# Convolution blocks inside the attention steps, up-projections ahead of the gating, low parts on VectorE: a two-layer trunk on one core

## The chip, the cores and the metric

The kernel runs on one core of one Trainium2 chip. The metric is the device time of one execution in microseconds; a lower time is better. TensorE (PE in the profile) multiplies matrices and loads weights (PEld), VectorE is DVE, ScalarE is ACT, GpSimd is POOL, SyncE (SP) issues the DMAs.

## What is computed

Two layers of one trunk run over 256 latent and 256 context tokens of 1024 features. Each layer has a half-step feed-forward block, a mixing stage and a second half-step feed-forward block, each behind an RMS norm with shift, scale and gate. The change lies in the mixing stage, which joins three groups:

```python
q_lat, kv_lat, k_pe, sg_in, cv_in = jnp.split(hn @ w_mix_in[l], splits, axis=-1)
q = mla_queries(q_lat, ...)                # rms_norm, up-projection, norm per head, rope
k, v = mla_keys_values(kv_lat, k_pe, ...)  # the same for keys; values
attn = latent_attention(q, k, v, kc, vc)   # 8 heads, 256 queries on 512 keys
sg = spatial_gating(sg_in, ...)            # gelu, norm of v by groups, w_spatial @ v + b, times u
cv = short_conv(cv_in, w_conv[l])          # b * conv3(c * x)
y = jnp.concatenate([rms_norm(attn, ...), rms_norm(sg, ...), rms_norm(cv, ...)], axis=-1)
h = h + mod_l[5] * (y @ w_mix_out[l])
```

In layer 0 the context tokens go through the same steps with their own attention (256 queries on 256 keys); in layer 1 they give keys and values alone.

## The kernel before

**Products.** All large products take their operands in two parts, high and low (`whi`, `wlo`, `xh`, `xl`), and three matmuls per product (`mm3` with weights stationary, L384 to L386, `mm3x` with tokens stationary, L389 to L391). They go to PSUM tiles of the tag `mm`, of which there are six; two more, `sm`, serve transposes and small sums.

**Weights.** The class `Weights` streams all weights in the order of their use. A load brings a raw tile; `pump` makes the high part on ScalarE (L125) and the low part (L126) on the engine that `W.low` names: "g" is GpSimd, "v" VectorE, "a" both in turn. Five pairs of parts exist (`SUBB`); a new one is prepared when the prefix of finished weights (`sub_pref`) allows. `SPARE` is room of one pair that attention uses for itself. `W.hold` stops preparation except where `W.pump(1)` asks for one. `W.low` is "g" from the end of the first feed-forward block to the start of the second.

**Order.** The schedule is the program's order on each engine (`manual_schedule`); semaphores are placed by data dependencies and by the reuse of tiles. A mixing stage runs: latents of keys and queries (`kv_lat`, `kv_ctx`, in layer 0 `q_ctx`), `k_prep` (rotation of the shared key part), `uv_lat` and `uv_ctx` (gating inputs; their end emits `v_norm`, the norm of the gating's v, tile by tile: square on ScalarE, sums on VectorE, square root on ScalarE, four scalings on VectorE, high part on ScalarE, low part on VectorE). Then conv blocks 0 to 3, `spatial`, conv blocks 4 and 5, `y_sg` (transposed gated features), `k_up`, `y_cv_stats` (statistics of the convolution's norm), `q_up`, `y_cv` (the normalised convolution). A conv block is 24 matmuls of 512 columns in layer 0 and 256 in layer 1; kinds 0, 1 and 2 (c, x, b) are evacuated by a ScalarE copy, by a product and three convolution operations on VectorE, and by a product with a square.

**Attention** is twelve steps `att(i)`. Step i makes the scores of head i-2 (`B`: maxima and bias on VectorE, exponentials on ScalarE, normalisation on GpSimd), the transposed probabilities of head i-3 (`C`), products with the values (`Dv`, two heads at a time) and the transposed queries and keys of head i (`A`). Step 0 begins with `v_up`; its evacuations (`v_evac`) follow in steps 1 and 2. Steps 9 to 11 begin the output projection (`mo_begin`), which needs the features of the gating and the convolution.

`k_up` evacuates a tile with one step's delay: `fin` of tile t follows the square root of tile t+1, and frees the tile's bank.

Of the kernel before, what the change touches and what calls it, by code (L numbers as in the profile page):

```python
# [39 lines left out]
# packed per-partition parameters: name -> columns for one layer  # L40
# [20 lines left out]
class Weights:  # L61
    """Streams weights in order: DRAM -> raw tile -> (high, low) float32r parts, ahead of their use.
    SPARE in the stream is room of one weight, left to other uses between its take and its done."""

    def __init__(self, nc, pool, raws):
# [18 lines left out]
        self.sub_fin = [False] * len(self.subs)  # L84
        self.sub_pref = 0
# [7 lines left out]
    def pump(self, preps=None):  # L93
        """Start the loads that have room, and prepare the parts (at most preps, when held back)."""
# [3 lines left out]
        while go:  # L98
# [8 lines left out]
            while left > 0 and self.prep_i < len(self.subs) and self.prep_i < self.sub_pref + SUBB:  # L107
# [67 lines left out]
def hybrid_trunk_kernel(ctx: ExitStack, tc: tile.TileContext, io: dict, out: bass.AP):  # L175
# [65 lines left out]
    # ---------------------------------------------------------------- weight specs  # L241
# [110 lines left out]
    def split_norm(src, dst_h, dst_l, rb, a, b=None, eng=None):  # L352
        """high and low parts of src * a * rb (+ b); returns the emission of the low part."""
# [17 lines left out]
    def staggered(makers):  # L371
        """runs emissions that return a follow-up, each follow-up one later"""
# [60 lines left out]
    # ---------------------------------------------------------------- FFN  # L433
    def ffn(l, which, ntok, tail, first=None):
        """tail(part): called by the last block to start the chain of what follows."""
# [28 lines left out]
        def first_two(W):  # L464
            """Blocks 0 and 1: the latent half while the norm of the context half is under way."""
# [147 lines left out]
    def boundary(l, i):  # L613
        """tail of the last block before norm i of layer l: work(0..2) is the ctx half in three parts."""
# [18 lines left out]
    # ---------------------------------------------------------------- mixing  # L633
    def mixing(l):
# [5 lines left out]
        def open_pools(W):  # L640
# [9 lines left out]
            st["row"] = per.tile([128, NROW], F32, name="row")  # L650
            SP.dma_start(out=st["row"], in_=io["row"][:, l])
            P["kvh"] = per.tile([128, 2, NTOK], F32R, name="kvh")
            P["kvl"] = per.tile([128, 2, NTOK], F32R, name="kvl")
# [9 lines left out]
            P["stok"] = P["guv"][:, :, 0:256]  # L663
            P["cvo"] = p1.tile([128, 2, NQ], F32, name="cvo")
# [948 lines left out]
```

## Time and profile before

| | us |
|---|---|
| median of 3 runs | 1778.43 |
| range of the runs | 1777.52 to 1781.66 |
| profiled execution (its span; the page gives no other time of it) | 1778.8 |

| engine | busy us | share of the span |
|---|---|---|
| TensorE, matmul | 1715.4 | 96% |
| TensorE, weight load | 1450.0 | 82% |
| VectorE | 1077.7 | 61% |
| ScalarE | 661.1 | 37% |
| GpSimd | 328.9 | 18% |

Layer 0's mixing stage lies between about 406 and 650 us of the span, layer 1's between about 1403 and 1580. A view of stretches gives, for each piece of the span, how long every engine was busy in it; a busy time below the length is waiting. The granted clock of TensorE stands beside it, 1.00 for 2.4 GHz and 0.50 for 1.2 GHz. The order in time gives single instructions, with the idle time before one and what ended it in the last brackets.

### The profile page before, as it was taken

How to read it: one execution, taken by the hardware profiler on the slowest of the kernel's cores; microseconds unless marked ns; L12 is line 12 of the kernel's file. 1: busy time of each engine (PE TensorE's matmuls, PEld its weight loads, DVE VectorE, ACT ScalarE, POOL GpSimd, SP SyncE). 2: the span in 40 equal slices, each digit the busy share in tenths (PEclk: the TensorE clock that was granted, in tenths of full speed). 3: DMA queues.
4: the chain of work that ended last, by engine and by line, in shares of the span. 5: the costliest groups of instructions: out<-in, count | busy, mean ns of one | idle time of the engine just before them, and what ended most of it. 6: DMA issues, size and time to landing. Idle time of an engine off the chain costs nothing.

```text
span 1778.8 us, 24162 instructions
## 1 busy us (share of the span) xinstructions
PE 1715.4 (96%) x9422; PEld 1450.0 (82%) x9422; DVE 1077.7 (61%) x1778; ACT 661.1 (37%) x1124; POOL 328.9 (18%) x210
## 2 busy tenths in 40 slices
PE   8999999999998999999999999999999987889999
PEld 6888888889876688888888888888888986589999
DVE  5667777635578475575766356576765577554332
ACT  4422223224457443222232242222222355554442
POOL 0000000004346522000000030000000165465442
PEclk9999999999999999999999999999999998899999
DMA  8545555523211124454555234454454242136553
GB/s 318 189 158 181 184 182 191 178 84 98 82 60 48 37 70 151 134 176 155 165 175 166 98 107 158 162 164 161 158 174 123 70 142 69 36 116 210 185 180 94
DMA packets 71395, 248.59 MB, mean 140 GB/s; under 512 B 8048, under 2 KB 9584, under 8 KB 71280
## 3 DMA queue, kind: packets, MB, share of 16 engines
q1 hardware_dynamic: 71136, 246.97, 42.3%
q8 instruction: 74, 1.21, 0.3%
q14 instruction: 41, 0.34, 0.1%
q10 hardware_dynamic: 144, 0.07, 0.0%
HBM read 245.96 MB, written 1.05 MB: 139 GB/s over the span
## 4 chain that ended last, share of the span: by engine, by line
PE 87%; DVE 7%; ACT 3%; issue 2%; POOL 1%; DMA 1%; ACTq 0%; POOLq 0%; DVEq 0%
PE mm L384 26%; PE mm L385 25%; PE mm L386 25%; PE mm L389 2%; PE mm L391 2%; PE mm L390 2%; PE sm L288 1%; ACT p L1130 1%; PE sm L1181 1%; DVE mx L1119 1%; PE mm L1363 1%; DMA raw<-in_w_ada 1%; DVE xl L361 1%; PE sm L1076 1%; PE mm L1158 1%
## 5 line engine op out<-in xcount | busy, mean ns | idle before, releaser
L384 PE MATMUL mm<-xh,whi 128*128 128x512 f32 (+1 forms) x1712 | 612.0, 358 | 6.5 <-DVE kvl L723 3.1
L385 PE MATMUL mm<-xl,whi 128*128 128x512 f32 (+1 forms) x1712 | 605.7, 354 | 4.0 <-DVE xl L361 3.4
L386 PE MATMUL mm<-xh,wlo 128*128 128x512 f32 (+1 forms) x1712 | 604.1, 353 | 1.8 <-POOL wlo L126 1.3
L125 ACT ACTIVATE whi<-raw 128x1024 fp32r<-128x1024 f32 (+1 forms) x334 | 339.1, 1020 | 486.3 <-PE mm L385 373.6
L126 POOL TENSOR_TENSOR wlo<-raw,whi 128x1024 fp32r<-128x1024 f32 (+3 forms) x112 | 258.1, 2318 | 1335.7 <-ACT whi L125 1320.3
L126 DVE TENSOR_TENSOR wlo<-raw,whi 128x1024 fp32r<-128x1024 f32 (+2 forms) x222 | 265.9, 1199 | 244.8 <-ACT whi L125 244.8
L384 PEld LDWEIGHTS mm<-xh,whi 128*128 128x128 f32 x1712 | 327.4, 191 | 63.9 <-issue 11.8
L385 PEld LDWEIGHTS mm<-xl,whi 128*128 128x128 f32 x1712 | 327.4, 191 | 48.2 <-DVE xl L361 4.5
L386 PEld LDWEIGHTS mm<-xh,wlo 128*128 128x128 f32 x1712 | 327.4, 191 | 45.6 <-POOL wlo L126 1.5
L278 DVE SCALAR_TENSOR_TENSOR scratch<-raw,cs,scratch 128x512 f32<-128x512 f32 x448 | 307.4, 745 | 0.0
L384 PE MATMUL mm<-gh,whi 128*128 128x512 f32 (+1 forms) x770 | 270.2, 351 | 0.0
L386 PE MATMUL mm<-gh,wlo 128*128 128x512 f32 (+1 forms) x770 | 267.1, 347 | 0.0
L385 PE MATMUL mm<-gl,whi 128*128 128x512 f32 (+1 forms) x770 | 267.0, 347 | 0.0
L454 ACT ACTIVATE gh<-sa 128x512 fp32r<-128x512 f32 (+1 forms) x88 | 50.9, 579 | 310.2 <-DVE sa L453 310.2
L384 PEld LDWEIGHTS mm<-gh,whi 128*128 128x128 f32 x770 | 145.8, 189 | 22.3 <-issue 4.9
L386 PEld LDWEIGHTS mm<-gh,wlo 128*128 128x128 f32 x770 | 145.8, 189 | 18.3
L385 PEld LDWEIGHTS mm<-gl,whi 128*128 128x128 f32 x770 | 145.9, 189 | 17.5
L276 DVE TENSOR_SCALAR scratch<-raw,cs 128x512 f32<-128x512 f32 x64 | 28.2, 484 | 148.9 <-PE sm L288 148.9
L455 DVE TENSOR_TENSOR gl<-sa,gh 128x512 fp32r<-128x512 f32 (+1 forms) x88 | 57.7, 656 | 56.8 <-ACT gh L454 56.8
L453 DVE TENSOR_TENSOR sa<-sa,mm 128x512 f32<-128x512 f32 (+1 forms) x88 | 53.9, 613 | 17.7 <-PE mm L386 16.0
L408 DVE TENSOR_TENSOR acc<-acc,sq 128x256 f32<-128x256 f32 x63 | 41.4, 657 | 35.1 <-ACT sq L407 35.1
L360 ACT ACTIVATE xh<-scratch,mods 128x256 fp32r<-128x256 f32 x88 | 42.8, 506 | 52.9 <-DVE scratch L356 52.9
(207 smaller groups left out, 1457.6 us busy)
## 6 DMA issues: line engine op xcount, KB each, us to landing
raw<-in_w_ffn_in SPq DMA_DIRECT2D x176, 512.0 KB, 3.9
raw<-in_w_ada SPq DMA_DIRECT2D x144, 512.0 KB, 4.2
raw<-in_w_ffn_out SPq DMA_DIRECT2D x64, 512.0 KB, 4.4
raw<-in_w_ffn_out SPq DMA_DIRECT2D x32, 384.0 KB, 3.4
raw<-in_w_mo SPq DMA_DIRECT2D x16, 512.0 KB, 3.5
raw<-in_w_cv SPq DMA_DIRECT2D x12, 512.0 KB, 3.7
raw<-in_w_uv SPq DMA_DIRECT2D x8, 512.0 KB, 3.9
raw<-in_w_q SPq DMA_DIRECT2D x8, 384.0 KB, 3.1
```

What stands on the lines that cost most here:

```text
L125: nc.scalar.activation(hi[:, a:b], src, AF.Copy)
L126: eng.tensor_tensor(lo[:, a:b], src, hi[:, a:b].bitcast(F32), ALU.subtract)
L278: DVE.scalar_tensor_tensor(acc[:, s], src, cv, acc[:, s], ALU.mult, ALU.add)
L360: ACT.activation(dst_h, u, AF.Identity, bias=b)
L384: PE.matmul(bank, lhsT=wh, rhs=xh, start=first, stop=False)
L385: PE.matmul(bank, lhsT=wh, rhs=xl, start=False, stop=False)
L386: PE.matmul(bank, lhsT=wl, rhs=xh, start=False, stop=last)
L389: PE.matmul(bank, lhsT=xh, rhs=wh, start=first, stop=False)
L408: DVE.tensor_tensor(acc[:, half], acc[:, half], sq, ALU.add)
L453: DVE.tensor_tensor(sa[:, 0:n], sa[:, 0:n], bb[:, 0:n], ALU.mult)
L454: ACT.activation(st["gh"][:, m, 0:n], sa[:, 0:n], AF.Copy)
L455: DVE.tensor_tensor(st["gl"][:, m, 0:n], sa[:, 0:n], st["gh"][:, m, 0:n].bitcast(F32), ALU.subtract)
```

## The change

The six conv blocks leave the stretch ahead of attention and become parts of steps 0 to 5; their weights follow `SPARE` in the stream. `y_sg` moves to step 6, `y_cv_stats` and `y_cv` to step 8. The order ahead of attention becomes `k_up`, `v_up`, `spatial`, `q_up`. After `uv` only the first tile of `v_norm` is emitted; `k_up` emits the others, one behind each of its tiles. `v_up` evacuates at once. `W.low` is "v" from `kv_ctx` on. Finished weights are counted (`sub_done`) in place of the prefix. `k_up`, `v_up`, `spatial`, `q_up` and steps 0 to 6 each ask for one preparation. Keys' latents, the row of gains and `pss` move to the pool that closes ahead of attention; the convolution's tiles move to the pool of attention; the gated features lie in the scratch tile. Comments and docstrings are emptied.

```diff
         def kv_ctx(W):
+            W.low = "v"
             b = tok_mm(P["kvs"], 288, (2, 3), True, W)
...
     def done(self, i):
-        self.sub_fin[i] = True
-        while self.sub_pref < len(self.subs) and self.sub_fin[self.sub_pref]:
-            self.sub_pref += 1
+        self.sub_done += 1
         self.pump()
...
-                v_norm((0, 1, 2, 3))
+                v_norm((0,))
...
-        def conv_block(i):
+        def conv_block(W, i):
             blk, kind = divmod(i, 3)
...
         def spatial(W):
             s, wh, wl = W.take()
+            P["stok"] = new_scratch()[:, 0:nq]
...
-        for i in range(6):
-            job(conv_block(i), [conv_spec[i // 2]] if i % 2 == 0 else [])
-            if i == 3:
-                job(spatial, sp_spec)
...
                 if last:
                     last()
                 last = fin
+                if t + 1 < nq:
+                    v_norm((t + 1,))
             last()
             W.done(s)
+            W.pump(1)
...
-                def evac(t=t, bk=bk):
-                    if t % 2:
-                        DVE.tensor_copy(P["v"][:, t], bk)
-                    else:
-                        ACT.activation(P["v"][:, t], bk, AF.Copy)
-                evacs.append(evac)
+                if t % 2:
+                    DVE.tensor_copy(P["v"][:, t], bk)
+                else:
+                    ACT.activation(P["v"][:, t], bk, AF.Copy)
             W.done(s)
-            P["v_evac"] = evacs
+            W.pump(1)
...
-        job(y_sg)
+            W.pump(1)
+
         job(k_up, ku_spec)
-        job(y_cv_stats)
+        job(v_up, vu_spec)
+        job(spatial, sp_spec)
         job(q_up, qu_spec)
-        job(y_cv)
...
                 if i == 0:
-                    v_up(W)
                     P["spare"] = W.take()
...
+                a = None
+                if i < 2:
+                    a = A(i)
+                    for f in a[0] + a[1]:
+                        f()
+                if i < 6:
+                    conv_block(W, i)
+                elif i == 6:
+                    y_sg(W)
+                elif i == 8:
+                    y_cv_stats(W)
                 late, evac = ([], []), []
                 if 0 <= i - 3 < H:
                     evac = C(i - 3)
...
                 P["late"] = late
-                if 1 < i < H - 1:
+                if i == 8:
+                    y_cv(W)
+                if i < H - 1:
                     W.pump(1)
...
         for i in range(H + 4):
-            job(att(i), vu_spec + [SPARE] if i == 0 else mo_spec(i - H - 1) if i > H else [])
+            cv = [] if i > 5 else conv_spec[i // 2][i % 2:i % 2 + 1]
+            job(att(i), ([SPARE] if i == 0 else []) + cv + (mo_spec(i - H - 1) if i > H else []))
```

## Rows read from the trace of the kernel before

**Rows 1.** First part of the page: busy time, share of the span, instructions.
```profile
PE 1715.4 (96%) x9422; PEld 1450.0 (82%) x9422; DVE 1077.7 (61%) x1778; ACT 661.1 (37%) x1124; POOL 328.9 (18%) x210
```

**Rows 2.** Stretches of layer 0: length, engines' busy time, PEclk, DMA share, GB/s.
```profile
464.60:498.80 34.20, 34.20 (x159) 28.48 (x158) 24.06 (x55) 16.32 (x38) 14.47 (x7) 1.00 0.30 100
...
527.60:560.60 33.00, 24.70 (x148) 19.63 (x147) 25.25 (x46) 24.51 (x58) 18.21 (x18) 0.90 0.11 38
...
560.60:599.30 38.70, 36.63 (x244) 27.34 (x242) 22.03 (x48) 23.86 (x58) 21.53 (x26) 1.00 0.07 24
...
466.00:486.00 20.00, 20.00 (x90) 16.52 (x88) 14.61 (x40) 9.46 (x20) 5.24 (x3) 1.00 0.18 61
...
573.50:578.90 5.40, 5.40 (x43) 4.46 (x41) 4.17 (x10) 4.16 (x12) 3.18 (x5) 1.00 0.02 5
```

**Rows 3.** The same view, stretches of layer 1.
```profile
1442.60:1495.40 52.80, 42.38 (x266) 38.09 (x265) 44.31 (x85) 25.32 (x57) 29.48 (x23) 0.94 0.34 112
...
1495.40:1521.50 26.10, 20.34 (x101) 14.08 (x100) 16.90 (x33) 17.30 (x37) 17.41 (x13) 0.80 0.18 61
...
1521.50:1550.40 28.90, 24.90 (x164) 18.42 (x162) 14.19 (x30) 14.78 (x33) 10.97 (x12) 0.94 0.06 19
...
1453.90:1459.60 5.70, 5.70 (x50) 5.70 (x49) 3.59 (x16) 3.28 (x7) 0.90 (x1) 1.00 0.00 0
...
1469.80:1476.60 6.80, 4.01 (x12) 3.25 (x13) 6.21 (x9) 2.06 (x5) 5.73 (x4) 0.50 0.59 191
...
1521.50:1524.50 3.00, 3.00 (x23) 2.62 (x21) 1.97 (x5) 1.60 (x4) 0.65 (x1) 1.00 0.36 115
...
1540.70:1542.60 1.90, 1.90 (x18) 1.08 (x17) 0.75 (x2) 1.28 (x4) 0.83 (x1) 1.00 0.00 0
```

**Rows 4.** Page, costliest groups: busy us, mean ns of one, idle before it.
```profile
L126 POOL TENSOR_TENSOR wlo<-raw,whi 128x1024 fp32r<-128x1024 f32 (+3 forms) x112 | 258.1, 2318 | 1335.7 <-ACT whi L125 1320.3
L126 DVE TENSOR_TENSOR wlo<-raw,whi 128x1024 fp32r<-128x1024 f32 (+2 forms) x222 | 265.9, 1199 | 244.8 <-ACT whi L125 244.8
```

**Rows 5.** Order in time, VectorE: start, length (us), line, operation, idle before it.
```profile
513.86 0.69 DVE L975 TENSOR_TENSOR k_tok<-mm,hr 128x512 f32<-128x512 f32 x1
...
1441.55 2.35 DVE L790 TENSOR_TENSOR gqk<-vec 128x1 f32<-128x1 f32 x1
...
1534.03 0.69 DVE L1119 TENSOR_REDUCE mx<-mm 128x1 f32<-128x512 f32 x1 [1.05 <-PE mm L391]
```

**Rows 6.** Order in time, TensorE, layer 1: two waits (last brackets).
```profile
1434.52 0.50 PE L390 MATMUL mm<-wlo,xh 128*128 128x512 f32 x1 [1.59 <-POOL wlo L126]
...
1472.59 0.47 PE L927 MATMUL mm<-ident,q_tok 128*128 128x128 f32 x1 [5.65 <-DVE q_tok L914]
```

**Rows 7.** Order in time, ScalarE, layer 0: squares of two tiles' gating norms.
```profile
468.34 0.40 ACT L819 ACTIVATE sa<-q_tok 128x256 f32<-128x256 f32 x1
...
471.12 0.40 ACT L819 ACTIVATE sa<-q_tok 128x256 f32<-128x256 f32 x1
```

**Rows 8.** The same view: squares of two tiles of k_up.
```profile
507.65 0.58 ACT L964 ACTIVATE sa<-mm 128x512 f32<-128x512 f32 x1
...
509.45 0.58 ACT L964 ACTIVATE sa<-mm 128x512 f32<-128x512 f32 x1
```

**Rows 9.** Order in time, TensorE, layer 0: q_up waits for a bank.
```profile
510.18 0.41 PE L389 MATMUL mm<-whi,qlh 128*128 128x384 f32 x1 [0.57 <-DVE k_tok L975]
```

**Rows 10.** Order in time, ScalarE: q_up's square roots, then a table load.
```profile
520.46 0.21 ACT L1028 ACTIVATE hm<-hm 128x8 f32<-128x8 f32 x1 [0.74 <-DVE hm L1027]
...
523.20 0.21 ACT L1028 ACTIVATE hm<-hm 128x8 f32<-128x8 f32 x1 [1.00 <-DVE hm L1027]
...
526.03 1.28 ACT L237 ACT_TABLE_LOAD   x1
```

**Rows 11.** Order in time, GpSimd: last rope of q_up; normalisation of a head.
```profile
525.01 0.74 POOL L1042 TENSOR_TENSOR q_tok<-q_tok,row 128x256 f32<-128x256 f32 x1 [1.87 <-ACT q_tok L1024]
...
1537.69 2.04 POOL L1138 TENSOR_TENSOR p<-p,rs 128x512 f32<-128x512 f32 x2 [2.50 <-DVE rs L1136]
```

More of the change, by code (lines that the diff above doesn't have):

```diff
@@ L83, in __init__ @@
         self.sub_t = {}
[L84 to L85 removed]
+        self.sub_done = 0
         self.prep_i = 0
@@ L106, in pump @@
                 go = True
-            while left > 0 and self.prep_i < len(self.subs) and self.prep_i < self.sub_pref + SUBB:
+            while left > 0 and self.prep_i < len(self.subs) and self.prep_i < self.sub_done + SUBB:
                 if self.subs[self.prep_i] is None:
@@ L649, in open_pools @@
             P["rqs"] = per.tile([128, nq, H], F32, name="rqs")
-            st["row"] = per.tile([128, NROW], F32, name="row")
+            st["row"] = p1.tile([128, NROW], F32, name="row")
             SP.dma_start(out=st["row"], in_=io["row"][:, l])
-            P["kvh"] = per.tile([128, 2, NTOK], F32R, name="kvh")
-            P["kvl"] = per.tile([128, 2, NTOK], F32R, name="kvl")
+            P["kvh"] = p1.tile([128, 2, NTOK], F32R, name="kvh")
+            P["kvl"] = p1.tile([128, 2, NTOK], F32R, name="kvl")
             P["qlh"] = p1.tile([128, 3, NQ], F32R, name="qlh")
@@ L790, in k_prep @@
             DVE.tensor_tensor(gqk, vcol(l, "gqn"), vcol(l, "gkn"), ALU.mult)
-            P["pss"] = per_t = P["per"].tile([128, 4], F32, name="pss")
+            P["pss"] = per_t = P["p1"].tile([128, 4], F32, name="pss")
             for t in range(4):
@@ new lines, in conv_block @@
+            s, wh, wl = W.take()
+            bk = mm_bank()
+            sl = slice(0, NQ)
+            for k in range(DK):
+                mm3(bk[:, sl], wh[:, 128 * k:128 * k + 128], wl[:, 128 * k:128 * k + 128],
+                    st["xh"][:, k, sl], st["xl"][:, k, sl], k == 0, k == DK - 1)
+            W.done(s)
+            ns = NQ // 256
+            v3 = lambda a: a[:, sl].rearrange("p (s t) -> p s t", s=ns)
+            if kind == 0:
+                P["c_sb"] = temp(512, "sa", 2)
+                ACT.activation(P["c_sb"][:, sl], bk[:, sl], AF.Copy)
+            elif kind == 1:
+                z = P["z"]
+                DVE.tensor_tensor(z[:, 0:ns, 1:257], v3(P["c_sb"]), v3(bk), ALU.mult)
+                y = P["y"]
+                w3 = [vcol(l, "w_conv", 3 * blk + j) for j in range(3)]
+                DVE.tensor_scalar(v3(y), z[:, 0:ns, 0:256], w3[0], None, ALU.mult)
+                DVE.scalar_tensor_tensor(v3(y), z[:, 0:ns, 1:257], w3[1], v3(y), ALU.mult, ALU.add)
+                DVE.scalar_tensor_tensor(v3(y), z[:, 0:ns, 2:258], w3[2], v3(y), ALU.mult, ALU.add)
+            else:
+                DVE.tensor_tensor(P["cvo"][:, blk], P["y"][:, sl], bk[:, sl], ALU.mult)
+                if blk == 0:
+                    ACT.activation(P["cacc"][:, sl], P["cvo"][:, 0], AF.Square)
+                else:
+                    sq = temp(512, "sa", 2)
+                    ACT.activation(sq[:, sl], P["cvo"][:, 1], AF.Square)
+                    DVE.tensor_tensor(P["cacc"][:, sl], P["cacc"][:, sl], sq[:, sl], ALU.add)
@@ L1063, in close_p1 @@
             P["p2"] = P["es2"].enter_context(tc.tile_pool(name=f"pb{l}", bufs=1))
-            P["at"] = P["p2"].tile([128, 4, NQ], F32, name="at")
+            p2 = P["p2"]
+            P["at"] = p2.tile([128, 4, NQ], F32, name="at")
+            P["cvo"] = p2.tile([128, 2, NQ], F32, name="cvo")
+            P["cacc"] = p2.tile([128, NQ], F32, name="cacc")
+            P["y"] = p2.tile([128, NQ], F32, name="cy")
+            z = P["z"] = p2.tile([128, NQ // 256, 258], F32, name="z")
+            DVE.memset(z[:, :, 0:1], 0.0)
+            DVE.memset(z[:, :, 257:258], 0.0)
             new_acc()
@@ L1206, in fn @@
                     bk, ctx_part = B(i - 2, lows)
-                    if i == 2:
-                        for f in P.pop("v_evac")[2:4]:
-                            f()
                 else:
```

55 lines of the change are left out of this document (8 added, 47 removed).

## The prediction

> **What bounds the kernel now.** The page's first part gives the reading order: TensorE is busy 96% of 1778.8 us [rows 1], so a change pays only where TensorE waits or runs at half clock. I then cut both mixing stages into stretches and compared TensorE's busy time with the length of each. In layer 0 the convolution and gating stretch has no wait at all (34.20 of 34.20), the first attention steps lose 8.3 of 33.0 with a granted clock of 0.90, the last steps 2.1 of 38.7 [rows 2]. In layer 1 the stretch before attention loses 10.4 of 52.8, the first attention steps 5.8 of 26.1 at 0.80, the last 4.0 of 28.9 at 0.94 [rows 3]. So the idle time is in the attention steps, and the six convolution blocks that move there stand in dense TensorE time of layer 0. The reader is to see that the blocks are good cover in both places: what matters is what stands bare where they are taken away.
>
> **The change part by part.**
>
> *Low parts on VectorE.* A low part costs VectorE 1.20 us and GpSimd 2.32 [rows 4]. While GpSimd makes low parts, tiny VectorE operations take as long as one of them: L790, one column, took 2.35 us [rows 5]. In layer 1 TensorE waits 1.59 us for such a part, and 5.65 us for the gated features, which queued behind stalled VectorE work [rows 6]. Both waits should go. VectorE has room before attention (44.3 of 52.8 busy, most of it those stalls) [rows 3]. I take 1.6 for the first; between 0 and 3 as bounds. The Trainium skill ("SBUF — State Buffer", Who interferes with whom) says that a VectorE instruction with two SBUF inputs and a GpSimd one that reads SBUF exclude each other for a whole instruction; the row agrees. It also speaks against the change, since the low part itself has two SBUF inputs: that is the first rival.
>
> *Layer 0 before attention.* The blocks hid a serial chain of ScalarE and VectorE. One tile's gating norm takes 2.78 us from square to square [rows 7], one tile of k_up 1.80 [rows 8]. Both alternate between the two engines, and the new order puts them into one queue, norm t+1 behind k_up's tile t: 4.6 us a tile. The first square of k_up is where the second norm's square stands now, 471.1 [rows 7]; the four tiles then end at 471.1 + 4 x 1.80 + 3 x 2.78 = 486.7, and the last k_up bank is free about 1.4 later, after two multiplications of 0.69 [rows 5], at 488.1. TensorE needs only 24 matmuls for k_up, 24 for v_up, at 0.227 (88 in 20.0 us [rows 2]): 11 us from 464.8. There are six mm banks: four go to k_up, two to v_up, and v_up's third tile waits for the first k_up tile to be evacuated, which is emitted behind the second. That this happens is seen now, where q_up waits for k_tok [rows 9]. Spatial waits for the last two banks and the last norm, and ends near 489, where unhindered it would end near 477: 12 us of wait. q_up then follows: ScalarE first makes spatial's four squares, its rstd and one high part, to about 495.9, and takes 2.6 us a tile on average (up to 2.74, square root to square root [rows 10]); the last tile's rope on GpSimd, 0.74 [rows 11], ends at 506.5. v_up, which covers this tail now, has been used up. Head 0's transposes start at 506.6 instead of 527.6. The removed TensorE work is 33.1 (six blocks of 24 x 0.23) and some 1.6 of transposes and statistics, so 13.7 of the 34.7 is lost to waits.
>
> *Layer 0, attention steps 0 to 5.* A step without waits takes 5.4 now (573.5 to 578.9, all busy [rows 2]), of which A is 0.85, B 2.16, C 1.4 and the short Dv 1.0; the long one has twice the matmuls, 1.95. With a block of 5.52 in each: 2 x 6.37, then 8.5, 2 x 9.95 and 11.9 make 53.0. VectorE has 25.3 us of work in some five steps now [rows 2]; with a low part and at most 2.7 of convolution it has 6 to 9 in steps of 8.5 to 12, so TensorE sets the pace. Coming out of a wait it runs at half clock for a while (12 matmuls in 6.8 us, clock 0.50 [rows 3]); I add 1.7, bounds 0 and 3.4. Step 6 starts at 506.6 + 54.7 = 561.3; now 560.6. So all that attention gains here, the front has lost.
>
> *Layer 0, steps 6 to 11.* No block is left, but y_sg, y_cv_stats and y_cv are added, and low parts on VectorE. Step 6 needs eight banks of six and about 8 us of VectorE: 8.0 for 7.0 now. In step 8 the broadcast of y_cv stands in TensorE's queue ahead of head 7's scores. It waits for the exponentials of head 6, a load of the square root's table (1.28 [rows 10]), two square roots, reciprocals and diagonals: about 5.4 after head 6's scores end, where head 7's begin 2.4 after them now: +3.0. The load back to exponentials delays the context half of head 6 by 1.4 and, with y_cv's six VectorE operations in front, head 7's by 2.0. With 0.25 won in step 7 for GpSimd's missing low parts: 1.0 - 0.25 + 3.0 + 1.4 + 2.0 is +7.2 for the tail. Bounds +2 (only the table chain) and +11. The Trainium skill ("ScalarE: Activation LUTs", What ACT_TABLE_LOAD costs) gives about 2.66 us a switch with its drain; the row has 1.28 for the load alone, and the sum goes by that. By that page two switches would make the tail 2.8 longer.
>
> *Layer 1.* Blocks have half the columns: 24 x 0.119 (48 in 5.7 us [rows 3]) is 2.9. uv ends at 1442.6; with key latents on ScalarE first and only two norms, k_up starts at 1445.4, by the same periods its four tiles end at 1461, the banks come free by 1462.7, spatial ends at 1465.9 (partly at half clock), q_up's ScalarE and rope at 1478.2; less the 1.6 above, A(0) at 1476.6 instead of 1495.4: -18.8. A, B and C take 3.0 [rows 3]; with 2.9 each and one Dv of 1.9: 2 x 3.6, 5.1, 2 x 6.0 and 7.9 make 32.3. Here VectorE comes close: its 16.9 us of the present four steps [rows 3], less some 2 of standing behind GpSimd, with four low parts (4.8) and 3 of convolution make 22.8 in the 25 us of steps 2 to 5, so I add 0.9, and 1.7 for the clock: 34.9, now 26.1: +8.8. In the tail head 5's scores no longer wait behind GpSimd's low part: -1.2. Now head 6's maxima start at 1534.03 [rows 5], its probabilities are ready at 1537.69 + 2.04 [rows 11]; with the square root's table between, head 7 comes 2.7 later. Layer 1: -18.8 + 8.8 + 1.5 = -8.5.
>
> *At nothing.* The done counter in place of the prefix, the pool that holds row and keys, z's memset and the gating's home in scratch lie beside waits longer than they are. On SP's queue the loads for k_up, v_up, spatial and q_up pass those of the convolution; the DMA engines are 0 to 0.34 busy there [rows 2, 3], and each part is prepared two jobs ahead of its use; if that cover is gone, a weight costs its low part's 1.2 [rows 4] and the high part before it. mo 3 is prepared in mo_head instead, beside three blocks of products. On GpSimd, y_cv's low parts queue behind a normalisation, and head 7's normalisation behind them, which step 8's 2.0 contains.
>
> *Sum.* Layer 0 +0.7 + 7.2 = +7.9, layer 1 -8.5: -0.6. A walk like this misses hops between engines; I add 2 (an estimate, bounds 0 and 5). That is +1.4 on the profiled span, which stands 0.4 above the runs' median of 1778.4: 1780 for the median.
>
> **The rivals.**
>
> *VectorE and GpSimd exclude each other (slower).* It decides if VectorE passes TensorE in the attention steps. Each step's low part and the convolution's operations may each wait for one normalisation, 1.02 (2.04 for two [rows 11]). Four such in steps 2 to 5 of layer 1 make 22.8 + 8 against 25, +6, and one a step in both tails +4, on the 1779 to 1780 above: 1789. For it: L790. Against it: GpSimd is idle half of each step once it makes no low parts.
>
> *The tails are covered (faster).* If the blocks let the probabilities run ahead, and step 8's wait for the square root lies beside ready work, layer 0's tail costs 1 instead of 7.2, layer 1's -1.2 instead of 1.5, and the added 2 fall away, 10.9 in all: 1769. For it: layer 0 has only 2.1 of waits there now [rows 2]. Against it: the broadcast stands in front of the scores in the same queue.
>
> *Nothing moves the end.* The waits are renamed, because the same engines' chains bound both orders: 1778.
>
> **How the numbers follow.** Forecast 1780, own range 1773 to 1787 (the bounds of tail, clock and hops, not all at one end), 0.45; contention 1789, 0.22; covered tails 1769, 0.25; renamed 1778, 0.08. A change of 0.2%, 3.6 us, is about what a measurement of this kernel can tell from none: 1774.9 to 1782.0. Of the forecast 0.05 lies below, 0.14 above. Faster 0.05 + 0.25 = 0.30, same 0.26 + 0.08 = 0.34, slower 0.14 + 0.22 = 0.36. The range for 8 in 10 is 1765 to 1792, which takes in the middle of each rival.
>
> **What would show it.** In layer 0 two or three TensorE waits of 3 to 5 us between k_up and spatial, ended by k_tok; A(0) near 507; steps 2 to 5 near 10 us without waits; step 6 near 561; two more table loads a layer, both in steps 8 and 9, and a wait of the broadcast behind diagonals. In layer 1 A(0) near 1477 and the end of attention some 8 earlier than now. Wrong, if v_up runs through without waiting (then 10 us faster), or if steps 2 to 5 are longer than the sum of their products.

## The result and the profile after

The changed kernel takes 1790.6 us (median of 4 runs, 1789.0 to 1790.7); the kernel before, on the same chip, 1778.0. The ratio is 1.0062, with a 95% interval of 1.0049 to 1.0076: slower by 0.6%, 11 us. The forecast of 1780 and its own range (1773 to 1787) missed the time; the range for 8 in 10 (1765 to 1792) holds it.

The page's first part (answers [rows 1]; its spans are 1788.8 now and 1778.8 before):

```profile
PE 1717.8 (96%) x9422; PEld 1454.5 (81%) x9422; DVE 1082.9 (61%) x1832; ACT 666.1 (37%) x1128; POOL 200.3 (11%) x152
```

TensorE has as many matmuls as before and is busy 2 us longer; 8 us more are idle. Where they are shows in the stretches (length, engines' busy time, PEclk, DMA share, GB/s). They answer [rows 2] and [rows 3]: layer 0 from k_up to head 0, steps 0 to 5, steps 6 to the statistics of the attention output; the same three of layer 1, from the end of uv; last, layer 1's output projection with the first steps behind it.

```profile
463.48:502.26 38.78, 28.82 (x135) 25.21 (x134) 29.11 (x79) 20.73 (x56) 7.89 (x13) 0.91 0.15 50
502.26:556.55 54.29, 52.53 (x294) 44.21 (x292) 35.77 (x68) 30.89 (x66) 13.37 (x16) 1.00 0.18 59
556.55:606.30 49.75, 41.57 (x264) 30.59 (x261) 27.65 (x63) 30.20 (x69) 21.01 (x25) 0.97 0.07 22
1448.70:1478.40 29.70, 24.14 (x111) 19.80 (x109) 21.68 (x54) 17.28 (x42) 4.79 (x8) 0.89 0.29 100
1478.40:1518.18 39.78, 34.73 (x244) 31.58 (x245) 26.98 (x50) 20.38 (x41) 8.46 (x10) 0.91 0.23 79
1518.18:1556.06 37.88, 28.97 (x173) 22.00 (x170) 21.94 (x46) 21.76 (x46) 13.18 (x14) 0.86 0.09 30
1556.06:1590.72 34.66, 25.49 (x169) 23.52 (x169) 20.87 (x40) 15.02 (x26) 1.46 (x2) 0.83 0.36 122
```

In layer 0 the blocks did in attention what was hoped: 52.5 of 54.3 busy at full clock, where 24.7 of 33.0 were before. Their old place has now 10.0 us of idle time. The last steps take 49.8 for 38.7; 8.2 of them idle, 2.1 before. In layer 1 head 4's scores come earlier than before, but the last steps take 37.9 for 28.9 and give nearly all of it back.

Since the front of a layer is not cut alike in both kernels, I compare all kernels below by five lengths (us, from the profiled runs): layer 0 from the first transposes of the normalised key latents to head 4's scores, and from there to the statistics of the attention output; layer 1 from the statistics ahead of its mixing stage to head 4's scores, and on to those of the attention output; last, from there to the statistics ahead of the last FFN.

```
kernel          ratio    L0 to 4  L0 rest  L1 to 4  L1 rest  L1 out
before          1         120.0     38.6    124.2     28.9    26.7
after           1.0062    117.0     49.8    113.8     37.9    30.1
a_low_g         1.0049    118.2     51.0    113.1     37.0    27.3
b_low_v         1.0000    121.5     36.8    116.7     33.3    29.3
a_cv_late       1.0004    117.0     42.8    112.0     33.7    30.0
a_no_sqrt       1.0031    117.0     45.9    113.7     36.0    30.1
a_bc9           1.0051    117.1     47.9    112.1     38.0    30.5
a_nosqrt_bc9    1.0027    117.1     45.6    112.1     33.9    30.1
a_front2        1.0080    118.5     50.0    111.8     39.6    29.4
best1           0.9992    118.1     44.1    112.2     33.4    27.6
best2           0.9986    117.0     43.9    112.4     34.1    27.3
best3           1.0043    122.8     43.6    115.8     34.9    28.3
best4           0.9964    112.4     44.1    110.3     35.0    27.5
best5           0.9934    112.5     42.8    107.9     34.7    27.3
```

After against before: -3.0 + 11.2 - 10.4 + 9.0 + 3.4 = +10.2, the difference of the profiled spans (10.0) within 0.2. Outside these stretches the two differ little: 1.1 less ahead of the first, 0.9 more behind the last. The stretches up to head 4 won 13 us, those behind it, with the output projection, lost 24. One profile is one execution: the seven kernels whose order up to head 4 is that of the changed one (after, the four with y_cv moved or its root left out, best1 and best2) lie at 117.0 to 118.1 in layer 0 and at 112.0 to 113.8 in layer 1, so a difference of 1 to 2 us in one stretch says little.

The main waits of the changed kernel, from TensorE's order in time (start, length, line, operation; the idle time before it and what ended it):

```profile
477.32 0.77 PE L386 MATMUL mm<-whi,kvh 128*128 128x512 f32 x1 [5.22 <-DVE k_tok L962]
481.95 0.47 PE L386 MATMUL mm<-whi,kvh 128*128 128x512 f32 x1 [1.74 <-DVE k_tok L962]
486.60 0.36 PE L381 MATMUL mm<-vnh,whi 128*128 128x256 f32 x1 [3.00 <-DVE hr L959]
504.51 0.31 PE L1070 MATMUL sm<-ident,q_tok 128*96 128x128 f32 x1 [1.75 <-POOL q_tok L1029]
...
576.03 1.23 PE L329 MATMUL sm<-ones,cacc 128*128 128x1 f32 x8 [1.76 <-DVE qTl L1077]
588.75 0.43 PE L1175 MATMUL mm<-pt,v 128*64 128x256 f32 x1 [3.76 <-ACT p L1124]
...
1524.02 0.63 PE L1152 MATMUL mm<-ident,p 128*128 128x128 f32 x4 [2.44 <-DVE qTl L1077]
1539.80 1.19 PE L346 MATMUL sm<-scratch,ones 128*128 128x256 f32 x2 [4.50 <-DVE scratch L340]
1586.12 0.98 PE L329 MATMUL sm<-ones,acc 128*128 128x1 f32 x4 [4.38 <-DVE acc L405]
```

The first four are the front's: v_up for two of k_up's banks, spatial for the third (the gating's last norm had ended at 484.61), head 0 for the rope. Behind head 4 the broadcast of y_cv at 1539.80 is the longest. ScalarE beside it shows both table loads:

```profile
1536.73 1.28 ACT L334 ACT_TABLE_LOAD   x1
1538.02 0.20 ACT L334 ACTIVATE st_m<-st_m 128x2 f32<-128x2 f32 x1
...
1541.55 0.81 ACT L355 ACTIVATE xh<-scratch 128x256 fp32r<-128x256 f32 x2 [2.84 <-DVE scratch L353]
1544.58 1.28 ACT L1124 ACT_TABLE_LOAD   x1 [2.22 <-DVE nb L1109]
1545.87 0.78 ACT L1124 ACTIVATE p<-mm,nb,rqs 128x512 f32<-128x512 f32 x1
```

The second load stands behind 2.22 us in which ScalarE did nothing: it carries the wait of the exponential that needs the table, so it starts when the maxima are there and not when ScalarE is free. The first load did not do that: it began at 1536.73, before its operand was there (VectorE's st_m, 1536.83 to 1536.96). And behind the waits at 1524.02 and 1539.80 TensorE ran at half its clock (1.2 for 2.4 GHz):

```profile
1524.60:1528.00 3.40, 3.40 (x12) 2.86 (x12) 2.16 (x5) 3.40 (x8) 2.04 (x2) 0.51 0.09 36
1538.30:1545.20 6.90, 5.40 (x18) 4.27 (x18) 4.67 (x10) 1.84 (x4) 1.80 (x3) 0.51 0.01 2
```

8.8 us of work at half clock cost 4.4 us. So layer 1's +9.0 is 4.9 of idle time (8.9 for 4.0, [rows 3]), by estimate 2.7 more of half clock (before, the granted clock of 0.94 over 28.9 us [rows 3] cost 1.7), and the rest is the work that moved here.

In layer 1's output projection VectorE comes too late. Its order in time up to the first residual, then one period, and last the first residual before:

```profile
1562.82 3.50 DVE L125 TENSOR_TENSOR wlo<-raw,whi 128x1024 fp32r<-128x1024 f32 x3 [1.10 <-ACT whi L124]
1566.23 0.48 DVE L396 SCALAR_TENSOR_TENSOR h<-mm,mods,h 128x256 f32<-128x256 f32 x1
...
1571.32 1.23 DVE L125 TENSOR_TENSOR wlo<-raw,whi 128x1024 fp32r<-128x1024 f32 x1 [0.53 <-ACT whi L124]
1572.46 0.48 DVE L396 SCALAR_TENSOR_TENSOR h<-mm,mods,h 128x256 f32<-128x256 f32 x1
1573.48 0.42 DVE L405 TENSOR_TENSOR acc<-acc,sq 128x256 f32<-128x256 f32 x1 [0.54 <-ACT sq L404]
1574.43 1.22 DVE L125 TENSOR_TENSOR wlo<-raw,whi 128x1024 fp32r<-128x1024 f32 x1 [0.53 <-ACT whi L124]
```

```profile
1557.80 0.48 DVE L399 SCALAR_TENSOR_TENSOR h<-mm,mods,h 128x256 f32<-128x256 f32 x1 [1.82 <-PE mm L386]
```

Three low parts, 3.50 us, stand ahead of the first residual: it comes 10.2 us after the statistics of the attention output (1556.06), where it came 7.4 after them before (1550.38). That is 2.8 of the 3.4 lost. Then follows a period of a low part, a residual, a wait for ScalarE's square, its sum, and a wait for the next high part: 3.11 us from low part to low part, four times in a row, where a block's products take 2.9. So VectorE does not catch up, and the statistics at 1586.12 wait 4.38 for the last sum, while TensorE had no wait in the 22 us of products ahead of them.

### The profile page after: what moved, and what is told of

The parts are those of the page before. It is cut to its first block, busy times and chain, and to the rows that moved or that the text cites. A ratio compares the mean times of both kernels' runs of the same rounds, so it can differ in the third digit from the quotient of the medians.

```text
span 1788.8 us, 24143 instructions
## 1 busy us (share of the span) xinstructions
PE 1717.8 (96%) x9422; PEld 1454.5 (81%) x9422; DVE 1082.9 (61%) x1832; ACT 666.1 (37%) x1128; POOL 200.3 (11%) x152
## 4 chain that ended last, share of the span: by engine, by line
PE 87%; DVE 5%; ACT 3%; issue 2%; DMA 1%; POOL 1%; ACTq 0%; SPq 0%; POOLq 0%; DVEq 0%
PE mm L381 26%; PE mm L382 25%; PE mm L383 25%; PE mm L388 2%; PE mm L386 2%; PE mm L387 2%; PE sm L285 1%; ACT p L1124 1%; DMA raw<-in_w_ada 1%; DVE mx L1113 1%; DVE wlo L125 1%; DVE xl L358 1%; DVE scratch L353 0%; PE sm L1070 0%; ACT whi L124 0%
## 5 line engine op out<-in xcount | busy, mean ns | idle before, releaser
L125 DVE TENSOR_TENSOR wlo<-raw,whi 128x1024 fp32r<-128x1024 f32 (+2 forms) x280 | 333.8, 1196 | 291.5 <-ACT whi L124 291.4
L125 POOL TENSOR_TENSOR wlo<-raw,whi 128x1024 fp32r<-128x1024 f32 (+2 forms) x54 | 125.8, 2335 | 1291.7 <-ACT whi L124 951.4
L404 ACT ACTIVATE sq<-h 128x256 f32<-128x256 f32 x63 | 26.3, 418 | 99.3 <-DVE h L396 99.3
L357 ACT ACTIVATE xh<-scratch,mods 128x256 fp32r<-128x256 f32 x88 | 42.8, 506 | 52.1 <-DVE scratch L353 52.1
```

The source lines that it names most:

```text
L125: eng.tensor_tensor(lo[:, a:b], src, hi[:, a:b].bitcast(F32), ALU.subtract)
L357: ACT.activation(dst_h, u, AF.Identity, bias=b)
```

## The experiments

Three theories were open. **The tails**: the norm of y_cv in step 8, with its broadcast ahead of head 7's scores and its two table loads, is what the change costs. **The front**: the waits ahead of spatial are the cost, since cover was taken away. **The engines**: low parts on VectorE, which excludes GpSimd, are the cost (the slower rival of the prediction). The runs come from several chips, each beside the kernel before on the same chip; where us are given for a ratio, they are its difference times 1778.

### Low parts alone, from both sides

In a_low_g the changed kernel keeps GpSimd; in b_low_v the kernel before gets the same line.

```diff
         def kv_ctx(W):
-            W.low = "v"
```

> The changed kernel with the low parts of the mixing stages' weights back on GpSimd, all else as changed. Theory (the change's cost sits in the broadcast of y_cv in step 8, in the bare front, and for 3.8 us in layer 1's output projection, where low parts now stand ahead of the residual on VectorE): the 3.8 us of the output projection come back, the wait of 1.6 us of layer 1's gating-value products for a GpSimd low part returns, and the attention steps of layer 1 lose some 2 us, since GpSimd has a low part of 2.3 us beside the normalisation of 2.0 in each; 1787 to 1792 us. Rival (VectorE and GpSimd exclude each other, and low parts on VectorE are what made the tails longer): the tails lose most of their 9 to 11 us a layer, 1776 to 1782 us.

> The kernel before with only the low parts moved to VectorE from the context half of the key latents up to the end of the mixing stage. Theory: 1.6 us won in layer 1's gating-value products and some of the 5.7 us wait for the gated features, 3 to 4 us lost in layer 1's output projection: 1774 to 1779 us. Rival (low parts on VectorE are the cause of the loss): 1783 to 1789 us.

Measured: 1787.6 us, ratio 1.0049 (1.0032 to 1.0066), and 1777.7 us, 1.0000 (0.9989 to 1.0011). The stretches of a_low_g from head 4's scores on, layer 0, layer 1, and its output projection:

```profile
558.40:609.44 51.04, 42.47 (x263) 31.91 (x262) 28.09 (x61) 30.27 (x69) 23.79 (x27) 0.93 0.06 21
...
1522.10:1559.10 37.00, 28.74 (x174) 22.22 (x171) 21.11 (x44) 21.52 (x44) 17.81 (x16) 0.86 0.08 29
1559.10:1586.30 27.20, 23.21 (x162) 22.00 (x162) 14.01 (x25) 12.77 (x21) 21.47 (x10) 0.87 0.39 134
```

With GpSimd as before, the tails are about as long as with VectorE (51.0 and 37.0 for 49.8 and 37.9). So the engines' theory falls as the cause of the tails. What comes back is the output projection, 27.3 for 30.1, where VectorE no longer makes a low part in front of each residual. In the kernel before, the line is worth nothing in sum for a reason that the table shows: layer 1 wins 7.5 up to head 4, loses 4.4 in the steps behind it and 2.6 in the output projection. Most of the 4.4 is clock: the same 164 matmuls were busy for 28.2 us, 24.9 before [rows 3], at a granted clock of 0.85 for 0.94, and 1.1 us more are idle. Why the clock was lower there is open. The steps behind head 4 in layer 1 of b_low_v:

```profile
1514.40:1547.70 33.30, 28.20 (x164) 19.80 (x162) 16.27 (x32) 15.27 (x34) 11.86 (x13) 0.85 0.05 16
```

### The norm of y_cv

Four kernels take the chain in step 8 apart. a_cv_late moves all of it behind the last exponentials, where the square root's table has to be loaded anyway; products with blocks 6 and 7 then follow those with 4 and 5.

```diff
-                elif i == 8:
+                elif i == H + 2:
                     y_cv_stats(W)
...
-                if i == 8:
+                if i == H + 2:
                     y_cv(W)
...
-            mo_mm(P["mob"][j], P["mo"][j], SC, sl, True, False)
+            mo_mm(P["mob"][j], P["mo"][j], SC[0:2], sl, True, False)
+            if j == 2:
+                for i in range(3):
+                    mo_mm(P["mob"][i], P["mo"][i], SC[2:4], sl, False, False)
```

> The changed kernel with statistics, broadcast and split of the convolution's features moved from step 8 to step 10, behind the last exponentials and behind the one load of the square root's table; the output projection's products with these two blocks go to the end of step 11, the number of products is the same. Theory (the broadcast in step 8 with its two table loads is what the tails cost): layer 1 loses the wait of 4.5 us and the half clock behind it, layer 0 the longer steps 8 and 9, in all 8 to 13 us: 1777 to 1783 us. Rival (the tails are long because VectorE and GpSimd are full or exclude each other): the wait moves to another place, 1786 to 1790 us.

Measured: 1779.0 us, ratio 1.0004 (0.9994 to 1.0014); 10.3 of the 11 us are gone. The two tails of this kernel:

```profile
556.50:599.30 42.80, 39.48 (x263) 29.70 (x260) 26.76 (x63) 27.07 (x67) 20.73 (x25) 1.00 0.08 26
...
1508.50:1542.20 33.70, 26.73 (x175) 20.11 (x172) 21.74 (x46) 19.04 (x44) 13.19 (x14) 0.95 0.09 32
```

Against the changed kernel TensorE's idle time falls from 8.2 to 3.3 and from 8.9 to 7.0, and its granted clock rises from 0.97 to 1.00 and from 0.86 to 0.95: the same work is 2.1 and 2.2 us shorter. The theory of the tails stands. (The profiled execution was 2.6 us below this run's median, so the profiled spans differ by 14 where the timing gives 10.) What remains over before is mostly work that moved here in layer 0 (42.8 for 38.6, of which 2.9 busy and 1.3 idle), and mostly waits in layer 1 (33.7 for 28.9, 1.8 busy and 3.0 idle). The longest of these, 2.44, stands in step 6, where y_sg takes banks; putting y_sg elsewhere, below, ended it but did not change the sum.

a_no_sqrt takes out the square root alone (the argument added to its statistics skips it), a_bc9 moves the broadcast behind head 7's scores and leaves the loads, a_nosqrt_bc9 does both.

```diff
-            P["cdg"] = [stats(P["cacc"], s, 256) for s in halves()]
+            P["cdg"] = [stats(P["cacc"], s, 256, False) for s in halves()]
...
+                elif i == 9:
+                    y_cv(W)
...
-                if i == 8:
-                    y_cv(W)
```

> The changed kernel without the square root in the norm of the convolution's features in step 8, so without the load of the square root's table there and the load back ahead of head 7's exponentials; it leaves out that root (the features are scaled by the reciprocal of the mean square). All else, the broadcast in front of head 7's scores too, as changed. Theory 1 (the two table loads of 1.28 us are the cost: one lies in the broadcast's wait, the other ahead of head 7's exponentials, which the last steps wait for): 3 to 4 us a layer, 1782 to 1785 us. Theory 2 (the place of the broadcast in TensorE's queue is the cost, the loads lie beside other work): less than 2 us in all, 1788 to 1791 us.

> The changed kernel with the broadcast and split of the convolution's features moved from the end of step 8 to step 9, behind head 7's scores; statistics and square root, with both table loads, stay in step 8. Theory 1 (table loads): the load back stays ahead of head 7's exponentials, and what the broadcast waited for is only covered by 1.4 to 2.2 us of scores: 1785 to 1789 us. Theory 2 (place in TensorE's queue): nearly all of what the move to step 10 gave comes from here too, 1779 to 1783 us.

> Both edits at once that were tried singly on the norm of the convolution's features: no square root in step 8 (it leaves out that root), and the broadcast behind head 7's scores. Alone the first gave 5.5 us against the changed kernel and the second 1.9, the move to step 10 10.3 (ratios to the kernel before on the same chip, times 1778). Theory 1 (two separate prices): the sum, 7.4 us, a ratio of 1.002, 1780 to 1783 us. Theory 2 (each alone leaves the wait that the other one's cost then fills; statistics in step 8 as such cost nothing): the whole 10 us, a ratio of 1.0005, 1777 to 1780 us.

Measured: ratios 1.0031 (1.0013 to 1.0050), 1.0051 (1.0034 to 1.0067) and 1.0027 (1.0018 to 1.0037). The wait of the broadcast in layer 1, in a_no_sqrt, then in a_bc9, then with both (4.50 in the changed kernel):

```profile
1536.88 0.77 PE L347 MATMUL sm<-scratch,ones 128*128 128x256 f32 x1 [3.31 <-DVE scratch L341]
```

```profile
1536.81 0.67 PE L346 MATMUL sm<-scratch,ones 128*128 128x256 f32 x2 [2.38 <-DVE scratch L340]
```

```profile
1533.10 0.67 PE L347 MATMUL sm<-scratch,ones 128*128 128x256 f32 x2 [1.21 <-DVE scratch L341]
```

Without the load the wait is 1.2 shorter, behind the scores 2.1, with both 3.3: as a wait the two prices add up. By their ratios both single runs lie where the theory of the loads had them (1783.5 in 1782 to 1785, 1787.1 in 1785 to 1789; the median of a_no_sqrt as it stands, 1786.3, lies between both theories). The theory of the place, with 1788 to 1791 and 1779 to 1783, falls. The loads are worth more (5.5 us in both layers), the place less (1.9, within the noise of the two ratios): in a_bc9 the load back still stands in front of head 7's exponentials with all of its 1.28, and layer 1's tail stayed as long (38.0 for 37.9), 1.2 less idle but 1.3 more busy. In layer 1 both together reach the length of a_cv_late (33.9 for 33.7), in layer 0 not (45.6 for 42.8): the statistics in step 8 still wait 1.76 there for a bank, as in the changed kernel. Timed, both together gave 6 us (the sum of two prices was forecast at 7.4, the whole at 10) where the profiled stretches say 10. Part of this is the execution that was profiled, the fastest of its ten and 2.4 below their median; and 1.7 of the 10 lies ahead of head 4 in layer 1, where the order of both kernels is the same.

### Cover for the front

a_front2 puts two convolution blocks back, between k_up and v_up; the other four go to steps 1 to 4.

```diff
         job(k_up, ku_spec)
...
+        NF, OF = 2, 1
+        for i in range(NF):
+            job(conv_ahead(i), conv_spec[i // 2][i % 2:i % 2 + 1])
         job(v_up, vu_spec)
...
-                if i < 6:
-                    conv_block(W, i)
+                if NF <= i + OF < 6:
+                    conv_block(W, i + OF)
```

> The changed kernel with the first two of the six convolution blocks put back ahead of attention, between the key and the value up-projection; the other four stand in steps 1 to 4. Theory (about 10 us of layer 0's front and some 5 of layer 1's are bare waits, and four blocks are enough for the attention steps): layer 0 gains 8 to 10 us, layer 1 up to 2: 1778 to 1783 us. Rival (cover is worth as much in attention as ahead of it, the waits of the first attention steps come back): 1787 to 1791 us.

Measured: 1792.4 us, ratio 1.0080 (1.0065 to 1.0095). My theory fell (1778 to 1783), and the time lies a little above the rival's 1787 to 1791 too. Layer 0's waits of the front:

```profile
488.99 0.47 PE L386 MATMUL mm<-whi,kvh 128*128 128x512 f32 x1 [2.99 <-DVE hr L965]
508.01 0.31 PE L1078 MATMUL sm<-ident,q_tok 128*96 128x128 f32 x1 [1.75 <-POOL q_tok L1033]
...
511.28 0.45 PE L1078 MATMUL sm<-ident,q_tok 128*96 128x128 f32 x1 [2.14 <-POOL q_tok L1035]
515.86 1.09 PE L1078 MATMUL sm<-ident,q_tok 128*96 128x128 f32 x4 [3.29 <-DVE qTl L1085]
```

The blocks fill most of the waits ahead of spatial, and the idle time comes back at the transposes of heads 0 and 1. This says that products do not end the front but ScalarE's and VectorE's serial work does, k_up's and the gating's norms, then spatial's and q_up's; cover in front of it only sets where TensorE stands still. The next kernels test that.

### The front's serial work, and a faster kernel

If that is so, what has to leave the front is the gating's norms. Two steps come first: best2 and best1 take a_cv_late and set low parts back to GpSimd from step 8 on; best2 also moves y_sg to step 8.

```diff
+                if i == H:
+                    W.low = "g"
```

> The kernel with the norm of the convolution's features in step 10, and with two more edits: low parts back on GpSimd from step 8 on (the output projection's weights), and the gated features' transposes in step 8 instead of 6, where no head is prepared any more. Theory: 3.3 us in layer 1's output projection and up to 2.4 us of the wait in layer 1's step 6, against the 1779 us of the kernel without them: 1773 to 1776 us. Rival (GpSimd's low parts give it back in layer 0's or layer 1's last steps, as when all low parts were on it): 1778 to 1781 us.

> The kernel with the norm of the convolution's features in step 10, and low parts back on GpSimd from step 8 on; the gated features' transposes stay in step 6. In the run with both edits layer 1's output projection came back to 27.3 us from 29.9, and the moved transposes changed no sum: layer 0's last steps were 1.1 longer, layer 1's 0.4. Theory (the low parts ahead of the residual on VectorE are what the output projection paid for, the transposes' place is worth nothing): 0.998 of the kernel before, 1774 to 1778 us. Rival (the gain of that run came from the transposes): 1779 to 1781 us.

Measured: 1778.0 us, ratio 0.9986 (0.9975 to 0.9997), and 1776.1 us, 0.9992 (0.9979 to 1.0006). Layer 1's output projection is back at 27.3 and 27.6. The wait for the residual's squares is 1.64 again, as in the kernel before; in best1:

```profile
1572.19 0.58 PE L329 MATMUL sm<-ones,acc 128*128 128x1 f32 x4 [1.64 <-DVE acc L405]
```

By its median best2 missed its forecast of 1773 to 1776, by its ratio (1775.5) it held it; best1's 1774 to 1778 held either way. The place of y_sg makes no difference that can be measured.

best3 then moves the gating's norms and spatial into steps 0 and 1, ahead of the first exponentials. The gating's values go to the attention output's buffer, the norms' results to one of the weights' buffers.

```diff
-                if t + 1 < nq:
-                    v_norm((t + 1,))
...
-        job(spatial, sp_spec)
...
                 if i < 2:
+                    v_norm(range(nq // 2 * i, nq // 2 * i + nq // 2))
+                if i < 6:
+                    conv_block(W, i)
+                if i < 2:
                     a = A(i)
...
+                if i == 1:
+                    spatial(W)
+                    W.done(P.pop("vns")[0])
+                    preload(AF.Exp)
```

> As the one with these three edits, and the norms of the gating values and the spatial products moved from ahead of attention into steps 0 and 1, ahead of the load of the exponential's table, with buffers of their own. Theory (the front is set by the serial work of ScalarE and VectorE, 15 us of k_up's and the gating's norms, not by a lack of products beside it; two convolution blocks and two heads' transposes are 12.7 us of cover in layer 0): head 0 is prepared some 10 us earlier in layer 0 and spatial waits 3 at most: 7 to 10 us in layer 0, 2 to 4 in layer 1: 1762 to 1768 us. Rival (the chain only moves: spatial, and the exponentials behind it, are waited for in steps 1 and 2): 1772 to 1779 us.

Measured: 1788.9 us, ratio 1.0043 (1.0026 to 1.0060). The forecast (1762 to 1768) failed, and its rival's (1772 to 1779) too, on a step that neither had:

```profile
493.76 0.50 PE L381 MATMUL mm<-xh,whi 128*128 128x512 f32 x1 [3.28 <-ACT whi L124]
...
504.66 0.50 PE L381 MATMUL mm<-xh,whi 128*128 128x512 f32 x1 [1.87 <-ACT whi L124]
...
514.95 0.39 PE L381 MATMUL mm<-whi 128*128 128x256 f32 x1 [1.34 <-ACT whi L124]
517.47 0.58 PE L383 MATMUL mm<-whi,wlo 128*128 128x256 f32 x1 [2.01 <-DVE wlo L125]
```

TensorE waits for weights: with two buffers taken out in step 0, the weights' parts came too late for the products that need them; by the reading on which the next run was built, the convolution's high parts were made only behind q_up's last tile in ScalarE's queue. best4 prepares one part more inside q_up and takes the spare buffer in step 3.

> As the last one, with the norms of the gating values and the spatial products in steps 0 and 1, as in the run that came to 1789 us, but with the weights' parts prepared earlier: there the convolution's first weights were made behind the last query tile, and TensorE waited in steps 0 to 2 for high and low parts, 11 us in layer 0 and 10 in layer 1. The spare buffer is now taken in step 3, where it was taken in step 0, and one more part is prepared inside the query up-projection. Theory (these waits were preparation alone, and the serial work of ScalarE and VectorE hides under two convolution blocks): they go, 1766 to 1773 us. Rival (ScalarE and VectorE are full there, the waits only change their names): 1778 to 1787 us.

Measured: 1771.5 us, ratio 0.9964 (0.9950 to 0.9978). That holds the forecast (1766 to 1773). The waits for weights are gone; one of 5.40 stays where spatial waits for the last norm (whose high part now lies in a weights' buffer and is named `whi`):

```profile
506.48 0.58 PE L381 MATMUL mm<-whi 128*128 128x256 f32 x1 [5.40 <-ACT whi L824]
```

best5 puts the third block in front of spatial, and both in front of head 0's scores.

> As the kernel of 1771 us, with the third convolution block and, behind it, the spatial products ahead of head 0's scores in step 2; they stood at the end of step 1, where TensorE waited 5.4 us in layer 0 and 3.9 in layer 1 for the last norm of the gating values. Theory (5.5 and 2.9 us of products are cover for that norm, and head 0's exponentials, which now come later, are not waited for, since another block stands ahead of their transposes): 4 to 7 us less, 0.992 to 0.994 of the kernel before, 1764 to 1768 us. Rival (head 0's probabilities become what TensorE waits for in step 3): within 2 us of 1771.

Measured: 1768.0 us, ratio 0.9934 (0.9919 to 0.9949), faster than both kernels by 0.7% and 1.3%. The forecast (a ratio of 0.992 to 0.994, 4 to 7 us less than best4) held: 3.5 us between the medians, which are of two chips, and 5.3 by the ratios. In layer 0 the rival holds in part: the wait moved from spatial to the fourth block, which needs a bank that head 0's exponentials hold, and the way to head 4 is as long as in best4 (112.5 for 112.4); layer 1 gained 2.4 there.

```profile
520.66 0.80 PE L381 MATMUL mm<-xh,whi 128*128 128x512 f32 x1 [6.08 <-ACT p L1118]
```

## Why the prediction was right and wrong

**Layer 0's front: right.** Two or three waits of 3 to 5 us, 12 in all, were forecast up to the end of spatial; 5.22, 1.74 and 3.00 came, ended by k_tok and hr. One tile of k_up and one norm share a queue at 4.6 a tile: k_up's square roots stand at 476.38, 481.01 and 485.65. Head 0's transposes began at 502.26, with 1.75 of waiting for the rope inside, where 506.6 was forecast (505.5 with the 1.1 by which this run reached the stage earlier). That 12 us had been lost with the blocks' cover was the wrong name for it, as a_front2 shows.

**Layer 0, steps 0 to 5: right.** Steps of 8.5, 9.95, 9.95 and 11.9 were forecast; head to head it was 8.4, 9.7, 9.8 and 11.8. The 1.7 for a half clock did not come. Head 4 was 3.0 earlier than before instead of 0.7 later: the last rope, which head 0 waits for, was done 1.0 earlier than forecast (504.51 and the 1.1, for 506.6), and from there to head 4 it took 52.0 for 54.7.

**Layer 1 up to head 4: the sum right, in part by luck.** -10.0 was forecast and -10.4 measured, but two misses of some 2 us cancel. TensorE waited for the last rope until 1481.39; the stage began 7.0 later than in the kernel before, so that is 1474.4 in the times of the prediction, which had 1476.6. From there to head 4 it took 36.8, not 34.9. The two stretches are steps 0 and 1 from head 0's first transposes, and steps 2 to 5:

```profile
1478.42:1490.92 12.50, 9.84 (x61) 9.61 (x61) 6.16 (x14) 7.08 (x12) 2.30 (x4) 0.73 0.12 44
1490.92:1518.18 27.26, 24.88 (x186) 21.97 (x185) 20.82 (x37) 13.28 (x28) 6.16 (x6) 1.00 0.29 96
```

Steps 2 to 5 took 27.3, where their products were 25.0 and the forecast 25.9. Their 2.4 of waits end with VectorE's qTl and kTl; by the prediction's own sign (steps longer than the sum of their products) this part was wrong.

**Layer 0's tail: right place, too small.** +7.2 forecast (bounds 2 and 11), +11.2 measured. Two table loads, the delayed exponentials of heads 6 and 7 and the crowded banks of step 6 are all there. By steps (head 4 to 5, 5 to 6, 6 to 7, and on) it was +1.8, 0.0, +4.0 and +5.3, where +1.0, -0.25, +3.0 and +3.4 were forecast. But the broadcast itself did not wait. Step 8 lost its 4.0 by a wait of the statistics for a bank (1.76 at 576.03) and by the work of statistics and broadcast; and behind head 7 the values' products waited, since its exponentials hold their bank, 3.76 at 588.75.

**Layer 1's tail: the step that failed.** +1.5 forecast, +9.0 measured, and this alone is most of the miss of 11 us. Three terms were wrong. The broadcast was priced at 2.7 for one chain; it waited 4.50, and then the products ran at half clock, which was counted in steps 0 to 5 and not here. The two banks that y_sg takes were priced in layer 0 and not in layer 1, where a head's queries take one of the six as well: a wait of 2.44, and half clock again. And the 1.2 that head 5 was to gain from GpSimd's missing low part did not show. With the norm of y_cv behind the last exponentials (a_cv_late) the tail is 4.2 shorter: the broadcast's wait is gone, the one of 2.44 is still there.

**Layer 1's output projection: not seen.** +3.4, put at nothing. Parts of the weights were to be made "beside three blocks of products". In layer 0 nothing behind the tail got longer, but layer 1's blocks are half as long, as the prediction itself says of the convolution's: there three low parts hold back the first residual, and VectorE's 3.11 a block, above the products' 2.9, leaves no room to catch up. With low parts on GpSimd it is 27.3 to 27.6 again (a_low_g, best1, best2). Of the 1.6 forecast upstream 0.9 came. For the 2 us of hops, an estimate, the runs show no term of their own.

**The rivals.** Exclusion of VectorE and GpSimd gave 1789, nearly the time that was measured, but mostly by another mechanism. Its +6 in layer 1's steps 2 to 5 were 2.3, and giving the low parts back to GpSimd leaves the tails as they are. The two engines do lengthen each other's instructions where they meet, but that is seldom: in layer 0's attention three of 16 normalisations of 256 columns took 1.47 to 1.68 us for 0.61, and in each layer two low parts of 1024 columns took 1.56 to 1.66 for the usual 1.22; each of these seven began while the other engine was at a low part or a normalisation. The means over the 16, before and after:

```profile
L1138 POOL TENSOR_TENSOR p<-p,rs 128x256 f32<-128x256 f32 x16 | 9.5, 612 | 0.0
...
L1132 POOL TENSOR_TENSOR p<-p,rs 128x256 f32<-128x256 f32 x16 | 12.3, 786 | 14.1 <-DVE rs L1130 11.0 <-PE sm L1070 3.1
```

A time that fits is not yet a cause. "The tails are covered" is refuted by the tails, "Nothing moves the end" by the time.

**The table load.** By the Trainium skill ("ScalarE: Activation LUTs", What ACT_TABLE_LOAD costs) a switch costs about 2.66 us, drain included; by an estimate from that figure two a layer would be 10.6 in all. This case's rows do not show the drain: the operation behind a load starts as soon as the load ends (1536.73 and 1.28, then 1538.02; 1544.58 and 1.28, then 1545.87). Taking out the loads and the root gave 5.5 us in the timing, give or take 4, where four loads of 1.28 are 5.1; the measurement decides for the row.

## What to carry to other kernels

Before work is moved as cover, ask what ends the stretch that it leaves and enters: here a serial chain on ScalarE and VectorE ended the front, and two blocks of products put back beside it only moved the wait, while moving the chain itself under the products gave 0.3%, and 0.6% with one more block in front of spatial. A step that interrupts a run of one activation function is priced by both of its table loads and by everything queued behind it on TensorE; put it where the table changes anyway. Price an added step in every layer separately: what hides beside 5.5 us of products doesn't beside 2.9. And a new wait can cost a stretch at half clock on top: those of 2.44 and 4.50 in layer 1's tail did, the one of 1.76 in layer 0's step 8 did not. Sums that come out right are worth a look at their parts: in layer 1 two misses cancelled.

## What was not expected of the hardware

A table load that the program does not ask for ahead of time can wait with the operation that needs it: ScalarE idle for 2.22 us, then 1.28 of load at 1544.58. It need not: the square root's load at 1536.73 began before its operand was written. The half clock behind waits was worth as much as half of the waits: in layer 1's tail 4.4 us beside 8.9 of idle time. And low parts on VectorE next to normalisations on GpSimd cost little: where one began while the other engine was at work it got longer, up to 1.66 us for 1.22 and 1.68 for 0.61, but this happened five times in layer 0's attention and twice in layer 1's.
